# A hybrid decoder block on one core: which tile a Strassen sum is written to, when a head's output is scaled and transposed, and the order of the first casts

## The chip, the cores and the metric

One core of one Trainium2 chip runs the whole kernel in one launch. The metric is the device time of that core in microseconds (us); lower is better. The core's engines are TensorE (PE, matmuls, with PEld for its weight loads), VectorE (DVE), ScalarE (ACT), GpSimd (POOL) and SyncE (SP), which issues most DMAs.

## The reference, cut to what matters

For one layer, x of 1024 tokens by 1024, all float32:

```python
proj = x @ w_in                        # [q | f | i | og | pool_v | gate_a | gate_b]
a = HGRN2(q, f, i) -> per-head RMSNorm * sigmoid(og) -> @ w_a
b = per-group linear(causal_mean_w(pool_v) - pool_v) * pool_scale
mix = (sigmoid(gate_a) * a + sigmoid(gate_b) * b) @ w_out
x = LN(alpha * x + mix)
x = LN(alpha * x + relu(x @ w_up)^2 @ w_down)
```

HGRN2 is a gated recurrence of 8 heads with a state of 128 by 128: `S_t = diag(f_t) S_{t-1} + k_t v_t^T`, `o_t = S_t^T q_t`. The change touches the product with `w_in`, the recurrence's outputs and the pairs of `w_a`.

## The kernel before

**Products.** Every float32 product is made of three matmuls: an operand is split into a high part (float32r, a cast on ScalarE, `w_part` L245 by `split` L124, L126) and a low part (source minus high, on VectorE, L127), and hi·hi, hi·lo and lo·hi are summed in PSUM (`prod` L207, matmuls L212, L214 and L215). A product over 512 rows is four times three matmuls of 128x128 by 128x512.

**Pairs.** `pair` (L267) makes two output blocks of 128 columns for both halves of the tokens by a Strassen scheme (Winograd's form): 7 products in place of 8. The tokens' sums (a11, a12, a22, s1 to s4) lie split in SBUF all the time. The weights come as four raw blocks b11, b21, b12, b22 (128x4x128, 256 KB each, `loaded_blocks` L231, loads L223) and a fifth tile t from the same ring of six buffers (`block_tile` L217). On VectorE: T3 = b22 − b12 in t (L284), T2 = t + b11 (L301), T1 = b22 − T2 (L316), T4 = b21 − T2 (L309). Each is split and used by one product, in the order b11, b21, T2, T3, T1, T4, b22 (with `twin`, for the pairs of `w_a`: T3, T4, T2, T1 in the middle). What a tile holds decides when its buffer comes free for the next pair's load. Evictions of the products go over ScalarE (`copied`, L275) and VectorE (`added`, L279).

**Start.** Twelve idle products (L433), then the transposes of the first tokens (`transposed` L166, matmul L170; `first_tokens` L183), their splits (`in_parts` L173, cast L131, low part L132), and the first block of weights in four rows (`parts` L495 by `split`), which come by three DMAs: row 1, row 2, rows 3 and 4. `onto_chain` (L507) runs the first product row by row (L501 to L503). Ahead of them stands a small block on the lower bounds `lb` and the gains `g_neg` (L440 to L449), with one exponential (L443).

**Recurrence beside the products.** TensorE's order is written out by hand (`manual_schedule`): after every product `run` (L379) takes one turn of the generator `recurrence` (L1037). The other engines' orders come from a scheduler, which takes the order of emission, the dependences and its own times. Per head there are two halves of 512 tokens, 8.5 turns for each half. In turn 0 of a half stand `outputs` of the half before (L1010: the load of og L618, the products, squares L1022, root L1023 with its table load, reciprocal L1024, scaling by four ScalarE instructions L1026) and the keys and scores of this half. In turn `TURN_BACK` = 4 stand `turn_outputs` of the half before (L1028: four transposes L1032, the gate L1034 into og's tile, then `put_output` L632), the `states` of this half (L993) and the load of the next half's values. The other turns each take a piece of `prepare` (L881). `put_output` stores og's tile with SyncE (L636, L638) and, for the heads whose sums need it, with accumulating DMAs of GpSimd (L640, `s<-og`). The tag og has one buffer, so the next half's load of og (L618, on SyncE) waits for all of these. At the end of the recurrence, turns also take products of the pool's weights (`pool_products` L737, by `beside` L788), whose weight parts are split into tiles of the recurrence's tags (tD, tE, tF, og).

Of the kernel before, what the change touches and what calls it, by code (L numbers as in the profile page):

```python
# [12 lines left out]
AF = mybir.ActivationFunctionType  # L13
ALU = mybir.AluOpType
# [9 lines left out]
CH = HALF // P  # L24
# [3 lines left out]
LINE = 16  # L28
NW = 10
PER_HALF = 8.5  # L30
TURN_BACK = 4
TURNS_AHEAD = 3
ORDER = (
    ("inputs", 1), ("pooled", 0), ("inputs", 2), ("gates", 0), ("output_gates", 2), ("inputs", 3), ("pooled", 1),
# [17 lines left out]
def tile_hybrid_block(  # L52
# [52 lines left out]
    def f(t):  # L105
        return t.bitcast(F32)
# [17 lines left out]
    def split(src, tile_of):  # L124
        hi, lo = tile_of(), tile_of()
        A.copy(hi, src)  # L126
        V.tensor_sub(lo, src, f(hi))  # L127
        return hi, lo

    def split_into(t, src):  # L130
        hi = A.copy(t[:, 0], src)  # L131
        return V.tensor_sub(t[:, 1], src, f(t[:, 0])), hi  # L132
# [22 lines left out]
    r = [None] * 8  # L155
    xp = {name: [None] * CH for name in ("a11", "a12", "a22", "s1", "s2", "s3", "s4")}

    made_last, made_hi = {}, {}

    @contextmanager  # L160
    def behind_parts(name):
# [10 lines left out]

    def in_parts(name, kp, src):  # L173
        xp[name][kp] = act_tile()
        made_last[name], made_hi[name] = (i.ins for i in split_into(xp[name][kp], src))


    xt = [[None] * CH for _ in range(3)]
# [1 line left out]
    def minus_sum(out, a, b):  # L180
        V.scalar_tensor_tensor(out, a, -1.0, b, ALU.mult, ALU.subtract)
# [60 lines left out]
    def w_tile():  # L242
        return wq.tile([P, CH, P], F32R, tag="w", name=nm("w"), bufs=NW)

    def w_part(src):  # L245
        return split(src, w_tile)

    n_c = [0]

# [17 lines left out]
    def pair(raw, rooms, takes, pz_tag="pj", twin=False, pc_tag="pj", turned=False):  # L267


        b11, b12, b21, b22, t = raw if len(raw) == 5 else (*raw, None)  # L270
        c, ps = {}, {}

        def copied(room, ps):
            t = room()
            A.copy(t, ps)  # L275
            return t

        def added(t, ps):
            V.tensor_add(t, t, ps)  # L279
            return t  # L280

        def make_t3():
            c["t"] = block_tile() if t is None else t
            V.tensor_sub(c["t"], b22, b12)  # L284

        def t3():
            if twin:
                make_t3()
            return w_part(c["t"])

        def t2():
            if not twin:
                make_t3()
                make_t2()
            return w_part(b11)

        def make_t2():
            if turned:
                minus_sum(b11, c["t"], b11)
            else:  # L300
                V.tensor_add(b11, c["t"], b11)  # L301

        def t4():
            if twin:
                make_t2()
            if turned:
                minus_sum(b21, b11, b21)
            else:
                V.tensor_sub(b21, b21, b11)  # L309
            return w_part(b21)  # L310

        def t1():
            if turned:
                minus_sum(b12, b22, b11)
            else:
                V.tensor_sub(b12, b22, b11)  # L316
            return w_part(b12)

        def p1(w):
            ps["a"] = ps_tile()  # L320
            prod(ps["a"], w, "a11", True)
            c[11] = copied(rooms[0], ps["a"])

        def p2(w):
            if pz_tag == "pj":
                ps["z"] = ps_tile()
            ps["c"] = ps_tile(pc_tag, 4 if pc_tag == "pj" else 2)
            prod(ps["c"], w, "a12", True)

        def p7(w):  # L330
            if pz_tag != "pj":
                ps["z"] = ps_tile(pz_tag, 2)
            prod(ps["z"], w, "s3", True)
            with tc.high_priority(PRIO):
                takes[0](added(c[11], ps["c"]))
                c[22] = copied(rooms[2], ps["z"])

        def p6(w):
            prod(ps["a"], w, "s2", False)
            with tc.high_priority(PRIO):  # L340
                c[21] = copied(rooms[1], ps["a"])
                if twin:
                    takes[2](added(c[21], ps["z"]))

        def p4(w):
            prod(ps["z"], w, "a22", False)
            if not twin:
                with tc.high_priority(PRIO):
                    takes[2](added(c[21], ps["z"]))

        def p5(w):
            prod(ps["a"], w, "s1", False)
            with tc.high_priority(PRIO):
                takes[3](added(c[22], ps["a"]))

        def p3(w):
            prod(ps["a"], w, "s4", False)
            with tc.high_priority(PRIO):
                takes[1](ps["a"])

        def t0():
            return w_part(b11)

        def b_21():
            return w_part(b21)

        def b_22():
            return w_part(b22)

        middle = (  # L370
            ((t3, p7), (t4, p4), (t2, p6), (t1, p5)) if twin else ((t2, p6), (t3, p7), (t1, p5), (t4, p4))
        )
        return tuple(
            ((operand,), ((operand, product),)) for operand, product in ((t0, p1), (b_21, p2), *middle, (b_22, p3))
        )
# [48 lines left out]
    with tc.tile_pool(name="xr", bufs=8, side="right", reuse_waits="tile") as xr:  # L424
# [12 lines left out]
        lb = const.tile([P, 8], F32, name="lb")  # L437
        one_lb = const.tile([P, 8], F32, name="one_lb")
        e01 = const.tile([P, 16], F32, name="e01")
        V.tensor_max(lb, prm[:, 0:8], prm[:, 8:16])  # L440
        V.tensor_sub(e01[:, 0:8], prm[:, 0:8], lb)
        V.tensor_sub(e01[:, 8:16], prm[:, 8:16], lb)
        A.activation(e01, e01, AF.Exp)  # L443
        V.tensor_add(lb, e01[:, 0:8], e01[:, 8:16])
        V.reciprocal(lb, lb)
        V.tensor_mul(lb, lb, e01[:, 0:8])
        V.tensor_scalar(one_lb, lb, -1.0, 1.0, ALU.mult, ALU.add)
        g_neg = e01[:, 0:8]
        V.tensor_scalar_mul(g_neg, g_col, -1.0)  # L449
        x_rows = [xr.tile([P, CH, D], F32, name=f"x{u}", bufs=1) for u in range(2)]  # L450
        for t in range(8):
            r[t] = x_rows[t // CH][:, t % CH]
# [42 lines left out]
        def parts(rows):  # L495
            return [split(row, row_tile) for row in rows]
# [59 lines left out]
            put(0, 1, c, t)  # L556

        first_tokens("a11", "tr", "tr", "hg", "hg")
        w = parts(b11)
        first_tokens("a12", "tr")  # L560
        onto_chain(w, "a11", True, copied(c11, c_late))
        with behind_parts("a11"):
            w = parts(b21)
# [81 lines left out]
    with tc.tile_pool(name="tmp", bufs=1, side="right", reuse_waits="tile") as tmp:  # L645
# [224 lines left out]
        def chunk(c):  # L870
            return slice(c * P, (c + 1) * P)
# [4 lines left out]
        class Half:  # L876
# [133 lines left out]
            def outputs(self):  # L1010

                self.og = loaded(ogd[self.h][self.u], lambda: tt("og"))
                o = ps_tile("hg", 2)
                for c in range(CH):
                    w, prev = chunk(c), self.prev(c)
                    PE.matmul(o[:, w], att[:, c], self.v[:, c], start=True, stop=prev is None)
                    if prev is not None:
                        PE.matmul(o[:, w], self.qi[:, w], prev, start=False, stop=True)
                ss = small("ss", [P, CH])
                self.on = on = tt("tH")  # L1020
                for c in range(CH):
                    A.activation(on[:, chunk(c)], o[:, chunk(c)], AF.Square, accum_out=ss[:, c : c + 1])  # L1022
                A.activation(ss, ss, AF.Sqrt, bias=eps_rms, scale=1.0 / P)  # L1023
                V.reciprocal(ss, ss)  # L1024
                for c in range(CH):
                    A.activation(on[:, chunk(c)], o[:, chunk(c)], AF.Copy, scale=ss[:, c : c + 1])  # L1026

            def turn_outputs(self):  # L1028

# [7 lines left out]
        def recurrence():  # L1037

            def half(n, before):
                return Half(*divmod(n, 2), before) if n < 2 * HEADS else None  # L1040

            now, old, at = half(0, None), None, 0.0
            now.load()
            for _ in now.prepare():
                yield
            for _ in range(TURNS_AHEAD):
                yield
            for n in range(2 * HEADS + 1):
                if old:
                    old.outputs()  # L1050
                if now:
                    now.turn_keys()
                    now.scores()
                yield
                if now:
                    now.far_queries()
                nxt = half(n + 1, now) if now else None
                pieces = nxt.prepare() if nxt else iter(())
                at += PER_HALF
                for turn in range(1, round(at) - round(at - PER_HALF)):  # L1060
                    if turn == TURN_BACK:
                        if old:
                            old.turn_outputs()
                        if now:
                            now.states()
                        if nxt:
                            nxt.load()
                    else:
                        next(pieces, None)
                    yield  # L1070
                for _ in pieces:
                    pass
                now, old = nxt, now
# [456 lines left out]
```

## Time and profile before

| what | us |
| --- | --- |
| three runs | 1464.39, 1465.24, 1468.95 (median 1465.24) |
| profiled execution | 1466.59 |
| its span, first to last instruction | 1464.9 |
| TensorE busy / weight loads | 1435.5 / 1188.4 |
| VectorE / ScalarE / GpSimd busy | 1100.1 / 759.0 / 107.6 |
| mean granted TensorE clock | 0.996 |

How to read the rows: in a timeline, start, duration, engine, line, operation, tiles as out<-in; in brackets the idle time of the engine ahead of the instruction and what ended it. In the list of waits: engine and line, what they waited for, total us, times, longest. An engine with q (SPq) is its queue of instructions. Tiles go without their numbers. In the row of a DMA the last number is the median us from issue to landing. TensorE's matmuls overlap in the rows, so their pace is read from start to start.

### The profile page before, as it was taken

The numbers are of one execution on the slowest core, as the hardware profiler recorded it, in microseconds if no ns is written. First come the engines' busy times: TensorE is split into PE (matmuls) and PEld (weight loads), VectorE is DVE, ScalarE is ACT, GpSimd is POOL, SyncE is SP. The second block draws the span as 40 slices with busy tenths as digits, with TensorE's granted clock in tenths as the row PEclk, the third lists the DMA queues.
The fourth block names the chain that finished last, engine by engine and source line by source line (L and its number), as shares of the span: only waits on it lengthen the run. The fifth ranks groups of instructions, "written<-read, shape, count | busy, mean of one in ns | idle before, by whom it ended". The sixth has DMA issues, their size and how long they took to land.

```text
span 1464.9 us, 20840 instructions
## 1 busy us (share of the span) xinstructions
PE 1435.5 (98%) x7377; PEld 1188.4 (81%) x7377; DVE 1100.1 (75%) x1807; ACT 759.0 (52%) x1383; POOL 107.6 (7%) x288
## 2 busy tenths in 40 slices
PE   8999999999999999999999999999999999999997
PEld 7788888788878888877788878888888888888886
DVE  4967886796797796477985598666666787777977
ACT  5545566655755655555542366555556443333435
POOL 0002011211211210000002100000000100000000
PEclk9999999999999999999999999999999999999999
DMA  7142245345435546788673135444447774445422
GB/s 259 58 137 87 73 126 169 80 134 155 109 87 146 142 116 184 211 300 286 204 232 113 61 99 180 144 154 148 157 148 261 280 262 142 166 132 170 129 72 115
DMA packets 187161, 228.15 MB, mean 156 GB/s; under 512 B 12176, under 2 KB 110512, under 8 KB 187056
## 3 DMA queue, kind: packets, MB, share of 16 engines
q1 hardware_dynamic: 181088, 212.91, 43.9%
q0 software_dynamic: 5184, 11.54, 4.0%
q10 hardware_dynamic: 784, 2.38, 0.5%
q8 instruction: 58, 0.95, 0.3%
q14 instruction: 47, 0.39, 0.1%
HBM read 149.70 MB, written 77.07 MB: 155 GB/s over the span
## 4 chain that ended last, share of the span: by engine, by line
PE 87%; DVE 6%; DMA 4%; issue 1%; ACT 1%; SPq 0%; DVEq 0%; POOL 0%; ACTq 0%
PE ps_pj L212 15%; PE ps_pj L215 14%; PE ps_pj L214 14%; PE ps_pj L1412 4%; PE ps_pj L1413 4%; PE ps_pj L1411 4%; PE ps_pj L114 2%; PE ps_pj L113 2%; PE ps_pj L115 2%; PE ps_tr L1412 1%; PE ps_tr L1413 1%; PE ps_tr L1411 1%; PE ps_sc L215 1%; DVE w L127 1%; PE ps_hg L215 1%
## 5 line engine op out<-in xcount | busy, mean ns | idle before, releaser
L212 PE MATMUL ps_pj<-act,w 128*128 128x512 f32 x1068 | 420.2, 395 | 10.8 <-ACT c L275 3.3
L215 PE MATMUL ps_pj<-act,w 128*128 128x512 f32 x1068 | 415.7, 391 | 1.3 <-DVE w L127 1.3
L214 PE MATMUL ps_pj<-act,w 128*128 128x512 f32 x1068 | 415.0, 390 | 0.0
L126 ACT CAST w<-raw 128x512 fp32r<-128x512 f32 x310 | 192.5, 622 | 278.1 <-PE ps_pj L214 201.7
L127 DVE TENSOR_TENSOR w<-raw,w 128x512 fp32r<-128x512 f32 x310 | 212.1, 686 | 92.8 <-ACT w L126 87.6
L212 PEld LDWEIGHTS ps_pj<-act,w 128*128 128x128 f32 x1068 | 200.7, 188 | 56.9 <-ACT c L275 4.6
L215 PEld LDWEIGHTS ps_pj<-act,w 128*128 128x128 f32 x1068 | 200.8, 188 | 45.2 <-DVE w L127 2.6
L214 PEld LDWEIGHTS ps_pj<-act,w 128*128 128x128 f32 x1068 | 200.8, 188 | 40.8 <-DVE act L132 0.2
L1373 ACT CAST act<-act 128x1024 fp32r<-128x1024 f32 x66 | 66.9, 1050 | 109.0 <-issue 35.0
L279 DVE TENSOR_TENSOR c<-c,ps_pj 128x512 f32<-128x512 f32 x95 | 64.8, 682 | 39.1 <-PE ps_pj L215 35.6
L1374 DVE TENSOR_TENSOR act<-act,act 128x1024 fp32r<-128x1024 f32 x66 | 79.5, 1220 | 18.5 <-ACT act L1373 17.4
L1413 PE MATMUL ps_pj<-act,act 128*128 128x512 f32 x240 | 93.0, 389 | 0.0
L1412 PE MATMUL ps_pj<-act,act 128*128 128x512 f32 x240 | 93.0, 389 | 0.0
L1411 PE MATMUL ps_pj<-act,act 128*128 128x512 f32 x240 | 92.5, 389 | 0.0
L275 ACT COPY c<-ps_pj 128x512 f32<-128x512 f32 x96 | 55.8, 581 | 3.1 <-issue 1.8
L284 DVE TENSOR_TENSOR raw<-raw,raw 128x512 f32<-128x512 f32 x43 | 29.6, 690 | 33.2 <-DMA raw<-in_w_in_dram 28.8
L1411 PEld LDWEIGHTS ps_pj<-act,act 128*128 128x128 f32 x240 | 45.0, 188 | 9.4
L1412 PEld LDWEIGHTS ps_pj<-act,act 128*128 128x128 f32 x240 | 45.0, 188 | 9.4
L1413 PEld LDWEIGHTS ps_pj<-act,act 128*128 128x128 f32 x240 | 45.0, 188 | 9.3
L1282 ACT ACTIVATE c<-c 128x512 f32<-128x512 f32 x61 | 38.5, 632 | 1.7
L1281 ACT ACTIVATE c<-c 128x512 f32<-128x512 f32 x46 | 29.1, 632 | 15.0 <-DVE c L279 15.0
L1367 DVE TENSOR_TENSOR act<-act,ps_pj 128x512 f32<-128x512 f32 x45 | 30.1, 682 | 6.0 <-PE ps_pj L1413 5.7
(416 smaller groups left out, 2680.5 us busy)
## 6 DMA issues: line engine op xcount, KB each, us to landing
h<-c SPq DMA_DIRECT2D x106, 256.0 KB, 2.7
raw<-in_w_in_dram SPq DMA_DIRECT2D x100, 256.0 KB, 3.3
act<-h SPq DMA_DIRECT2D x78, 256.0 KB, 3.0
draw<-in_w_down_dram SPq DMA_DIRECT2D x16, 1024.0 KB, 7.6
raw<-in_w_up_dram SPq DMA_DIRECT2D x56, 256.0 KB, 2.8
hf<-h SPq DMA_DIRECT2D x34, 256.0 KB, 3.0
s<-og POOLq DMA_DIRECT2D x28, 256.0 KB, 6.1
v<-v SPq DMA_DIRECT2D x16, 256.0 KB, 3.3
```

The costliest lines, as they stand in the source:

```text
L126: A.copy(hi, src)
L127: V.tensor_sub(lo, src, f(hi))
L212: PE.matmul(ps, wh[:, k], th, start=first and k == 0, stop=False, skip_group_check=True)
L214: PE.matmul(ps, wh[:, k], tl, start=False, stop=False, skip_group_check=True)
L215: PE.matmul(ps, wl[:, k], th, start=False, stop=k == CH - 1, skip_group_check=True)
L275: A.copy(t, ps)
L279: V.tensor_add(t, t, ps)
L1373: A.copy(hi, src)
L1374: V.tensor_sub(lo, src, f(hi))
L1411: PE.matmul(ps, hh[:, w], wh, start=fresh and n == 0, stop=False, skip_group_check=True)
L1412: PE.matmul(ps, hh[:, w], wl, start=False, stop=False, skip_group_check=True)
L1413: PE.matmul(ps, hl[:, w], wh, start=False, stop=n == M - 1, skip_group_check=True)
```

## The change

Three edits.

1. In `pair`, T2 is written over b12 (its last reader until then was T3) and no longer over b11, and T1 into t's tile and no longer over b12; T4 and T1 read T2 from b12's tile. The number of instructions is the same.
2. The scaling of a half's outputs (four times L1026) is emitted in turn 2 (`TURN_SCALE`), behind the last cast of weights that was emitted, in place of turn 0; the transposes, the states and the load of values come in turn 5 in place of 4.
3. At the start only two rows of the first block are split before the first tokens; rows 3 and 4 are split behind the parts of the second and the fourth of the tokens' tiles, and the block on `lb` and `g_neg` stands behind the tokens' parts.

```diff
-TURN_BACK = 4
+TURN_BACK = 5
+TURN_SCALE = 2
...
+    last_hi = [None]
+
     def w_part(src):
-        return split(src, w_tile)
+        hi, lo = w_tile(), w_tile()
+        last_hi[0] = A.copy(hi, src).ins
+        V.tensor_sub(lo, src, f(hi))
+        return hi, lo
...
-            return w_part(b11)
+            return w_part(b12)
 
         def make_t2():
             if turned:
-                minus_sum(b11, c["t"], b11)
+                minus_sum(b12, c["t"], b11)
             else:
-                V.tensor_add(b11, c["t"], b11)
+                V.tensor_add(b12, c["t"], b11)
 
         def t4():
             if twin:
                 make_t2()
             if turned:
-                minus_sum(b21, b11, b21)
+                minus_sum(b21, b12, b21)
             else:
-                V.tensor_sub(b21, b21, b11)
+                V.tensor_sub(b21, b21, b12)
             return w_part(b21)
 
         def t1():
             if turned:
-                minus_sum(b12, b22, b11)
+                minus_sum(c["t"], b22, b12)
             else:
-                V.tensor_sub(b12, b22, b11)
-            return w_part(b12)
+                V.tensor_sub(c["t"], b22, b12)
+            return w_part(c["t"])
...
         first_tokens("a11", "tr", "tr", "hg", "hg")
-        w = parts(b11)
+        w = parts(b11[:2])
+        for row, kp in zip(b11[2:], (1, 3)):
+            lo_done, hi_done = made_kp["a11", kp]
+            with tc.issue_after(lo_done), tc.issue_after(hi_done):
+                w += parts([row])
+        with behind_parts("a11"):
+            V.tensor_max(lb, prm[:, 0:8], prm[:, 8:16])
...
+            A.activation(e01, e01, AF.Exp)
...
         first_tokens("a12", "tr")
...
-                for c in range(CH):
-                    A.activation(on[:, chunk(c)], o[:, chunk(c)], AF.Copy, scale=ss[:, c : c + 1])
+                self.o, self.root = o, ss
+
+            def scale_outputs(self):
+
+                with tc.issue_after(last_hi[0]):
+                    for c in range(CH):
+                        w = chunk(c)
+                        A.activation(self.on[:, w], self.o[:, w], AF.Copy, scale=self.root[:, c : c + 1])
...
                 for turn in range(1, round(at) - round(at - PER_HALF)):
+                    if turn == TURN_SCALE and old:
+                        old.scale_outputs()
                     if turn == TURN_BACK:
```

In the changed kernel the lines of the recurrence stand 11 further down up to the scaling and 17 from the transposes on: T3 is L290, the cast and the low part of weights L250 and L251 (others L127 and L128), the reciprocal L1035, the scaling L1043, the gate L1051.

More of the change, by code (lines that the diff above doesn't have):

```diff
@@ L156, in tile_hybrid_block @@
     xp = {name: [None] * CH for name in ("a11", "a12", "a22", "s1", "s2", "s3", "s4")}
-    made_last, made_hi = {}, {}
+    made_last, made_hi, made_kp = {}, {}, {}
     @contextmanager
@@ L174, in in_parts @@
         xp[name][kp] = act_tile()
-        made_last[name], made_hi[name] = (i.ins for i in split_into(xp[name][kp], src))
+        made_last[name], made_hi[name] = made_kp[name, kp] = [i.ins for i in split_into(xp[name][kp], src)]
     xt = [[None] * CH for _ in range(3)]
@@ L439, in tile_hybrid_block @@
         e01 = const.tile([P, 16], F32, name="e01")
[L440 to L449, printed above, removed]
         x_rows = [xr.tile([P, CH, D], F32, name=f"x{u}", bufs=1) for u in range(2)]
@@ L558, in tile_hybrid_block @@
         first_tokens("a11", "tr", "tr", "hg", "hg")
-        w = parts(b11)
+        w = parts(b11[:2])
[5 more added lines that the diff above has]
+            V.tensor_max(lb, prm[:, 0:8], prm[:, 8:16])
+            V.tensor_sub(e01[:, 0:8], prm[:, 0:8], lb)
+            V.tensor_sub(e01[:, 8:16], prm[:, 8:16], lb)
+            A.activation(e01, e01, AF.Exp)
+            V.tensor_add(lb, e01[:, 0:8], e01[:, 8:16])
+            V.reciprocal(lb, lb)
+            V.tensor_mul(lb, lb, e01[:, 0:8])
+            V.tensor_scalar(one_lb, lb, -1.0, 1.0, ALU.mult, ALU.add)
+            g_neg = e01[:, 0:8]
+            V.tensor_scalar_mul(g_neg, g_col, -1.0)
         first_tokens("a12", "tr")
```

## The prediction

> **What bounds the kernel now.** I read the page's busy shares and chain first, then what TensorE (PE) waited for, then the timeline around each of those waits.
>
> ```profile
> PE 1435.5 (98%) x7377; PEld 1188.4 (81%) x7377; DVE 1100.1 (75%) x1807; ACT 759.0 (52%) x1383; POOL 107.6 (7%) x288
> PE 87%; DVE 6%; DMA 4%; issue 1%; ACT 1%; SPq 0%; DVEq 0%; POOL 0%; ACTq 0%
> ```
>
> TensorE is the bound: busy 98% of the span and 87% of the chain that ended last. The change moves no matmul out of the program: in both instruction orders TensorE has the same 6149 rows. So it can only gain or lose where TensorE stands still or runs at a slower clock. Those places, with the engine that released them:
>
> ```profile
> PE ps_pj L212 <- ACT c L275: 3.3, 3, 1.6
> PE ps_pj L212 <- ACT w L126: 2.7, 2, 2.2
> PE ps_pj L212 <- DVE f L279: 2.0, 2, 1.3
> PE ps_pj L501 <- ACT act L131: 2.0, 1, 2.0
> PE ps_pj L212 <- ACT f L275: 1.5, 1, 1.5
> ```
>
> Columns: total us, times, longest. These are single events of 1 to 2 us. L501 is the first product of the kernel, the L275 and L279 rows are in the recurrence, and L126 (2.2) is its end. The steady pace, and three of the events:
>
> ```profile
> 431.24 0.39 PE L214 MATMUL ps_pj<-act,w 128*128 128x512 f32 x1
> 431.46 0.39 PE L215 MATMUL ps_pj<-act,w 128*128 128x512 f32 x1
> 433.32 0.50 PE L212 MATMUL ps_pj<-act,w 128*128 128x512 f32 x1 [1.47 <-ACT f L275]
> 437.62 0.50 PE L212 MATMUL ps_pj<-act,w 128*128 128x512 f32 x1 [1.29 <-DVE f L279]
> 319.77 0.50 PE L212 MATMUL ps_pj<-act,w 128*128 128x512 f32 x1 [0.74 <-DVE f L279]
> ```
>
> Start to start is about 0.227 us (431.24 to 431.46), so a product of 12 matmuls takes 2.72 us. The step 431.46 to 433.32 is 1.86 us, a loss of 1.63. In the same way each event is read as its step less 0.227.
>
> **The change part by part.**
>
> *First rows of weights behind first tokens.*
>
> ```profile
> 7.87 0.62 ACT L126 CAST w<-b 128x512 fp32r<-128x512 f32 x1 [1.82 <-DMA b<-in_w_in_dram]
> 9.27 0.66 PE L170 MATMUL ps_sc<-ident,x 128*128 128x128 f32 x4 [1.28 <-DMA x<-in_x_dram]
> 9.76 0.60 PE L170 MATMUL ps_hg<-ident,x 128*128 128x128 f32 x4
> 10.60 1.14 ACT L126 CAST w<-b 128x512 fp32r<-128x512 f32 x2 [2.12 <-DMA b<-in_w_in_dram]
> 11.64 0.21 ACT L443 ACTIVATE e<-e 128x16 f32<-128x16 f32 x1
> 11.76 1.05 ACT L131 CAST act<-ps_tr 128x512 fp32r<-128x512 f32 x2
> 12.38 0.50 PE L501 MATMUL ps_pj<-w,act 128*128 128x512 f32 x1 [2.02 <-ACT act L131]
> ```
>
> The transposes of the first tokens were done by 10.36, but ScalarE (ACT) stood for 2.12 us in front of the casts of rows 3 and 4, which wait for their DMA, and had the exponential next. In the changed order the four token casts come right behind row 2's cast (7.87 to 8.49). At 0.52 each (two in 1.05) the first is done near 9.1. The first product then waits only for the transposes ahead of it on TensorE, the last four from 9.76: four at the 0.123 that their predecessors took (9.27 to 9.76, four) end at 10.25. Gain: 12.38 − 10.25 = 2.1. Rows 3 and 4 are needed by the third and fourth quarters of the chain, 24 matmuls after 10.25, that is 15.7 at the earliest; their data is there at 10.60, so they are hidden. The exponential's result is used by the gates long after. The gap also costs clock:
>
> ```profile
> 12.40:16.60 4.20, 4.20 (x12) 0.59 1.05 390
> 16.60:21.00 4.40, 4.40 (x24) 1.00 1.05 387
> 13.24 0.63 PE L502 MATMUL ps_pj<-w,act 128*128 128x512 f32 x1
> 13.67 0.63 PE L501 MATMUL ps_pj<-w,act 128*128 128x512 f32 x1
> ```
>
> The windows show PE busy, granted clock (0.59 in the first), DMA share and GB/s. From 13.24 the products follow each other at 0.43 and not 0.227 until about 16.6: eight at 0.2 more, 1.6 us. The idle stretch from 10.36 to 12.38 lies just before. After the change nothing is idle from 9.27 on, so I count these 1.6 too: together **−3.7**, bounds −3.7 and −2.1.
>
> The Trainium skill (TensorE: Matmul & The Clock Gate, "What's actually happening") says that the clock is halved after an idle window of some 3.4 us and restored after a busy one, and that these windows run free of the kernel's start. The slow stretch here, 13.24 to 16.6, is as long as one such window. By that rule the stretch should go with the gap; where a window falls otherwise it could stay, and the sum would then lack the 1.6.
>
> *T2 over b12, T1 over t's tile.* No instruction is added; the tiles alone differ. b11's buffer comes free once T2 is computed, well before T4, so the next pair's b21 load is issued sooner. But T3 of the next pair needs b12 and b22, and these now wait for T1's and T4's readers, where they did before. The wait that reaches TensorE:
>
> ```profile
> DVE raw L284 <- DMA raw<-in_w_in_dram: 28.8, 16, 4.5
> SPq L618 <- DMA s<-og: 50.1, 15, 7.6
> 280.79 0.69 DVE L284 TENSOR_TENSOR raw<-raw,raw 128x512 f32<-128x512 f32 x1 [3.46 <-DMA raw<-in_w_in_dram]
> 287.94 0.88 ACT L1026 ACTIVATE tH<-ps_hg,ss 128x128 f32<-128x128 f32 x3 [0.41 <-DVE ss L1024]
> 289.36 0.50 PE L212 MATMUL ps_pj<-act,w 128*128 128x512 f32 x1 [1.62 <-ACT c L275]
> ```
>
> SyncE's queue stands at the load of the next half's og (L618) until the accumulating DMAs of the half before have landed, 50.1 us in all, and the block loads behind it stand too. VectorE then stands at T3 (3.46) and is late with everything behind: the reciprocal, hence the scaling L1026, hence the eviction L275 that TensorE needs at 289.36 (1.62 idle, and 0.16 beside it as at 433.32: 1.8 lost). In the changed order both block loads of this pair (at 277) stand ahead of the og load: T3 loses its wait of some 3 us, and this loss goes: **−1.8** (bounds −1.8 and 0).
>
> *Scale two, transposes one product later.* The scalings move little in ScalarE's list, behind the last cast of weights. The transposes, L1034, its puts and its accumulating DMAs come one product, 2.72 us, later, and with them the release of og's only buffer and SyncE's next og load. Where a block load stands behind that load, T3 is later:
>
> ```profile
> 395.58 0.69 DVE L284 TENSOR_TENSOR raw<-raw,raw 128x512 f32<-128x512 f32 x1 [0.76 <-DMA raw<-in_w_in_dram]
> 421.53 0.69 DVE L284 TENSOR_TENSOR raw<-raw,raw 128x512 f32<-128x512 f32 x1 [2.33 <-DMA raw<-in_w_in_dram]
> L638 SPq DMA_DIRECT2D s<-og x16: 339/447/764, 181.9 to 382.7; - x16
> ```
>
> At both, the changed order has one load behind the og load where there were two. That last load goes out 2.72 less one issue on SyncE later (0.45, the median of a put of this size in the last row), 2.2 to 2.3 us. It lands beside one transfer less: 256 KB at the 387 GB/s of full queues (the windows above) are 0.7. T3 is then, by this estimate, some 1.5 later. VectorE is busy without a break from there to 437, so the two evictions at 433.32 and 437.62 share one delay: **+1.5** (bounds −2.9, both losses gone, and +4.3, that is 2.7 and a slow stretch of 1.6). At 319.77 the last load falls behind puts of og that come 2.72 later, of which the slack of the load before hides more than half: **+0.5** (−0.7 to +1.1). The first of the losses on L275 has no load behind it: 0.
>
> *The end of the recurrence.* og's last DMAs free the tile into which the pool's weights are split:
>
> ```profile
> 608.97 0.74 DVE L1034 SCALAR_TENSOR_TENSOR og<-ps_tr,e,og 128x512 f32<-128x512 f32 x1
> 610.00 2.62 POOL L640 DMA_DIRECT2D s<-og  x3 [25.82 <-DVE og L1034]
> 620.52 0.69 DVE L127 TENSOR_TENSOR og<-tC,tF 128x512 fp32r<-128x512 f32 x1 [2.31 <-DMA s<-og]
> 621.51 0.39 PE L115 MATMUL ps_tr<-w,og 128*128 128x512 f32 x1
> 627.71 0.62 ACT L126 CAST tD<-tC 128x512 fp32r<-128x512 f32 x1 [3.37 <-DMA tC<-in_w_pool_dram]
> 628.90 0.50 PE L212 MATMUL ps_pj<-act,w 128*128 128x512 f32 x1 [2.16 <-ACT w L126]
> 630.30 0.50 PE L215 MATMUL ps_pj<-act,w 128*128 128x512 f32 x1 [0.67 <-DVE w L127]
> 631.69 0.63 PE L212 MATMUL ps_pj<-act,w 128*128 128x512 f32 x1
> s<-og POOLq DMA_DIRECT2D x28, 256.0 KB, 6.1
> ```
>
> Here pool products stand among the turns, so one turn is a product and six more matmuls, 2.72 + 1.4 = 4.1 us. L1034 comes at about 613.1, and if its DMAs take as long as before (608.97 to 620.52) the tile is free at 624.6 and its split done at 625.3; TensorE wants it at 621.51. That is a new wait of up to 3.8, and queued behind the split on VectorE are the next parts of weights and the evictions. Against it, the changed order casts the weights that TensorE missed at 628.90 ahead of tD's cast, so their 3.37 of waiting leaves that path: −2.2 and −0.7 (their idle time). Together 3.8 − 2.9 = +0.9 if the DMAs take as long as before, and −2.9 if they land in time; I take **0**, with the slow stretch behind them (0.63 for a matmul at 631.69, as at the start, 1.6 us) unchanged. Bounds: +3.8, and −2.9 − 1.6 = −4.5 if each DMA takes no more than the median 6.1 from its issue: three issues end near 615, plus 6.1 is 621.
>
> The Trainium skill (DMA: Bandwidth & Descriptors, "Anatomy of one DMA") prices such a DMA at 2.0 us and its bytes at 436 GB/s, 2.6 us for 256 KB. By that the new wait would not exist. The median above, 6.1, is more than twice that, and the measurement decides.
>
> What follows (states, v's load, the puts) hides under the next half's 8.5 products. The operands loaded after 675 change their order on SyncE: 0, between −2 and +2.
>
> **Sum.** −3.7 − 1.8 + 1.5 + 0.5 + 0 = **−3.5 us**. Against the profiled execution, 1466.6 (its span of 1464.9 and 1.7 around it, which stays), that is 1463.1. This one was 1.4 above the median of 1465.24, and against the median it gives **1461.7**.
>
> **The rivals.**
>
> 1. *The accumulating DMAs land at the median.* Then TensorE waits for nothing at the end: −4.5 instead of 0, a sum of −8.0, 1457.2. With the losses near 435 gone as well it is 1455 or less. For it: the median 6.1. Against: the last three, issued in 2.62 from 610.00, landed at 620.5, so the last took 7.9 or more.
>
> 2. *The later release becomes the bound* (slower). Price: each og load holds up the block loads behind it by the full 2.72. Then the 1.8 is not won, the two evictions lose 2.7 and a slow stretch of 1.6, the place at 319.77 loses 1.1 and the end 3.8: −3.7 + 4.3 + 1.1 + 3.8 = +5.5, and +2 with a late operand behind it: 1471 to 1473. It decides from the point at which the DMAs of the last half land later than 620.8, where TensorE at 621.51 misses its tile. For it: SyncE's 50.1 us at this very wait. Against: at 277 the order puts both loads ahead.
>
> 3. *The slow stretch at the start stays*, or falls elsewhere: −1.9, 1463.3. The rule on the clock above would allow it.
>
> 4. *The change does not do what it says at the start*: the first products wait for something else near 12.3, and only the rest remains: 1465.
>
> **How the numbers follow.** Forecast 0.42, rival 1 0.20, rival 2 0.17, rival 3 0.14, rival 4 0.07. A measurement of this kernel can tell about 0.3%, 4.4 us, from no change. Rival 1 and somewhat under half of the forecast's spread (its sum lies 0.9 inside that bound) are faster: 0.39. Rival 2 is slower: 0.17. The rest is within 0.3%: 0.44. The range leaves out the far ends of rivals 1 and 2: 1455 to 1470.
>
> **What would show it.** The start: first product (L497) near 10.3, no granted clock under 0.9 behind it. The waits: DVE's total for L290 under 28.8, with the 3.46 at 280 gone; SyncE's wait for s<-og longer than 50.1. Near 435: T3 and the two evictions later. At the end: VectorE's wait for s<-og, 2.3 before, several us, and the wait on L127's cast gone. The forecast is wrong if the first product is not earlier, if the DVE wait for s<-og stays near 2.3 (rival 1), or if TensorE shows new waits of over 2 us in several halves (rival 2).

## The result and the profile after

The change made the kernel slower: 1473.57 us median of 8 runs (1470.57 to 1476.92) against 1465.1 of 8 runs before (1462.62 to 1468.95), ratio 1.0055 with a 95% interval of 1.0039 to 1.0070. I had forecast 1461.7, and the time lies 3.6 above the range. The profiled execution took 1470.65, one of the two fastest, so its rows show less than the median loss: its last matmul starts 4.1 us later than before's. Its mean granted clock was 0.995, the median of the eight runs is 0.993. TensorE has 7377 matmuls in both profiles.

The start came as forecast. From the timeline of the changed kernel (weights' row 2, token casts, last transposes, first product), and its windows (PE busy, granted clock, DMA share, GB/s):

```profile
8.04 0.62 ACT L127 CAST w<-b 128x512 fp32r<-128x512 f32 x1 [2.98 <-DMA b<-in_w_in_dram]
8.57 1.06 ACT L132 CAST act<-ps_tr 128x512 fp32r<-128x512 f32 x2
9.95 0.60 PE L171 MATMUL ps_hg<-ident,x 128*128 128x128 f32 x4
10.31 0.48 PE L497 MATMUL ps_pj<-w,act 128*128 128x512 f32 x1
```
```profile
12.40:16.60 4.20, 4.20 (x21) 1.00 1.05 389
```

The first product starts at 10.31 in place of 12.38, and the clock between 12.4 and 16.6 is 1.00 in place of 0.59, with 21 matmuls in place of 12. What TensorE waits for afterwards (total us, times, longest):

```profile
PE ps_pj L213 <- ACT w L250: 8.8, 2, 7.3
PE ps_pj L213 <- ACT c L281: 4.6, 4, 2.0
PE ps_pj L213 <- ACT f L281: 1.6, 1, 1.6
PE ps_pj L213 <- DVE c L285: 1.4, 2, 1.1
PE ps_pj L213 <- DVE f L285: 0.5, 1, 0.5
```

The waits on the evictions of tile c by ScalarE (L281) did not go: 3.3 before, 4.6 now. And a single wait of 7.3 on ScalarE's cast of weights is new. It stands at the end of the recurrence:

```profile
611.54 2.63 POOL L651 DMA_DIRECT2D s<-og  x3 [25.57 <-DVE og L1051]
613.13 0.32 SPq L629 DMA_DIRECT2D c<-o  x1
613.54 0.42 SPq L629 DMA_DIRECT2D tH<-po  x1
622.09 0.62 ACT L127 CAST w<-tH 128x512 fp32r<-128x512 f32 x1 [11.45 <-DMA tH<-po]
623.28 0.80 PE L213 MATMUL ps_pj<-act,w 128*128 128x512 f32 x1 [7.29 <-ACT w L250]
```

A pooled operand (tH<-po) is loaded while the three accumulating DMAs are under way. ScalarE stands in front of its cast for 11.45 us, and the cast of weights that TensorE needs is next in ScalarE's queue. I had priced a wait here, but on another tile (og's) and on VectorE.

### The profile page after: what moved, and what is told of

It reads as the page before. It is cut to its first block, busy times and chain, and to the rows that moved or that the text cites. A ratio compares the mean times of both kernels' runs of the same rounds, so it can differ in the third digit from the quotient of the medians.

```text
span 1468.9 us, 20879 instructions
## 1 busy us (share of the span) xinstructions
PE 1435.8 (98%) x7377; PEld 1188.3 (81%) x7377; DVE 1099.8 (75%) x1807; ACT 758.7 (52%) x1383; POOL 105.5 (7%) x288
## 4 chain that ended last, share of the span: by engine, by line
PE 78%; DMA 7%; DVE 6%; issue 5%; ACT 3%; SPq 1%; POOL 0%; DVEq 0%; ACTq 0%; POOLq 0%
PE ps_pj L213 13%; PE ps_pj L215 13%; PE ps_pj L216 13%; PE ps_pj L1432 3%; PE ps_pj L1431 3%; PE ps_pj L1430 3%; DMA draw<-in_w_down_dram 2%; PE ps_pj L115 2%; PE ps_pj L114 2%; PE ps_pj L116 2%; PE ps_hg L215 1%; PE ps_sc L213 1%; PE ps_sc L215 1%; PE ps_sc L216 1%; PE ps_hg L213 1%
## 5 line engine op out<-in xcount | busy, mean ns | idle before, releaser
L213 PE MATMUL ps_pj<-act,w 128*128 128x512 f32 x1068 | 421.3, 395 | 17.4 <-ACT w L250 8.8
L250 ACT CAST w<-raw 128x512 fp32r<-128x512 f32 x303 | 187.8, 622 | 278.2 <-PE ps_pj L215 201.8
L251 DVE TENSOR_TENSOR w<-raw,w 128x512 fp32r<-128x512 f32 x303 | 207.1, 686 | 98.9 <-ACT w L250 97.2
L213 PEld LDWEIGHTS ps_pj<-act,w 128*128 128x128 f32 x1068 | 201.4, 189 | 64.7 <-ACT w L250 9.7
L281 ACT COPY c<-ps_pj 128x512 f32<-128x512 f32 x96 | 55.9, 582 | 6.6 <-PE ps_pj L216 3.3
L290 DVE TENSOR_TENSOR raw<-raw,raw 128x512 f32<-128x512 f32 x43 | 29.6, 689 | 32.8 <-DMA raw<-in_w_in_dram 27.6
L651 POOL DMA_DIRECT2D s<-og x28 | 24.9, 1162 | 144.1 <-DVE og L1051 144.1
```

What stands on the lines that cost most here:

```text
L213: PE.matmul(ps, wh[:, k], th, start=first and k == 0, stop=False, skip_group_check=True)
L250: last_hi[0] = A.copy(hi, src).ins
```

## The experiments

Ratios are against before on the same chip, with 95% intervals; the median of before in these batches was 1467.4, 1466.2, 1467.6 and 1466.6. Unless said otherwise a kernel is the changed one with the lines shown.

| kernel | median us | ratio (interval) |
| --- | --- | --- |
| start_alone | 1463.43 | 0.9970 (0.9961 to 0.9979) |
| tiles_alone | 1466.95 | 0.9995 (0.9983 to 1.0006) |
| turns_alone | 1479.19 | 1.0076 (1.0061 to 1.0090) |
| all_but_back | 1463.38 | 0.9968 (0.9957 to 0.9979) |
| last_back_4 | 1474.09 | 1.0051 (1.0036 to 1.0066) |
| last_only_5 | 1463.80 | 0.9980 (0.9970 to 0.9990) |
| no_last_puts | 1474.16 | 1.0049 (1.0035 to 1.0063) |
| back_3 | 1465.98 | 0.9994 (0.9984 to 1.0005) |
| outputs_4 | 1465.03 | 0.9983 (0.9972 to 0.9995) |
| outputs_5 | 1478.50 | 1.0066 (1.0048 to 1.0085) |
| no_adds_5 | 1461.11 | 0.9951 (0.9933 to 0.9969) |
| no_adds_4 | 1461.03 | 0.9954 (0.9938 to 0.9971) |
| plain_5 | 1463.30 | 0.9977 (0.9967 to 0.9987) |
| og_one_5 | 1476.51 | 1.0063 (1.0049 to 1.0076) |
| og_two_5 | 1474.41 | 1.0049 (1.0033 to 1.0065) |
| og_two_4 | 1473.18 | 1.0039 (1.0027 to 1.0050) |

**Which of the edits.** My first theory: the loss is the later turn, by its collision at the end of the recurrence. Rival: the tiles move the block loads.

start_alone is before with the third edit alone, tiles_alone with the first alone, turns_alone with the second alone; all_but_back is the changed kernel with

```diff
-TURN_BACK = 5
+TURN_BACK = 4
```

> Only the edit of the start. Both theories: the gap ahead of the first product and the slow clock behind it go, as in the changed kernel (first product near 10.3, no slow stretch to 16.6), and nothing else has a reason to move: 3.7 us less than before, about 1461.4. If the scheduler moves something else, the time differs from that.

> Only the edit of the tiles (T2 over b12, T1 over t's tile). Theory (the loss of the changed kernel lies in the later transposes, which meet the loads of the pool's operands at the end of the recurrence): no loss here, within 1.5 us of before, ScalarE's wait for tH<-po at the end 4 us as before. Rival (the tiles change the times of the block loads, and with them SyncE's order and the end): 5 us or more slower, with a wait of ScalarE for tH<-po of 8 us or more.

> Only the edit of the turns (scaling in turn 2, transposes, states and load in turn 5). Theory: the whole loss is here: the time of the changed kernel plus the 3.7 that the start gains there, 8 to 12 us slower than before, with one wait of TensorE of some 7 us at the end of the recurrence. Rival: at most 3 us slower, none over 4 us.

> The changed kernel with the transposes back in turn 4; the start, the tiles and the scaling in turn 2 stay. Theory: the end is as before (ScalarE's wait for tH<-po 4 us, none of 11), the start's gain stays: 1460 to 1463. Rival: still slower than before, 1468 or more.

The start gains 4.0 (1467.4 to 1463.4), the tiles give nothing that can be told from zero, the turns cost 11.8. Turn 4 in place of 5 alone takes the changed kernel to 1463.4, so the scaling in turn 2 costs nothing that can be told from zero, and the later transposes, states and load are the whole loss. The rival of the tiles falls.

**Is it the end?**

```diff
# last_back_4: the last half alone in turn 4
-                    if turn == TURN_BACK:
+                    if turn == TURN_BACK - (n == 2 * HEADS):
# last_only_5: TURN_BACK = 4, the last half alone in turn 5
+                    if turn == TURN_BACK + (n == 2 * HEADS):
# no_last_puts
-        for name in ONTO[right, u]:
+        for name in ONTO[right, u] if (h, u) != (HEADS - 1, 1) else ():
# back_3
+TURN_BACK = 3
```

> The changed kernel, with only the last half's transposes one turn earlier (turn 4); all other halves keep turn 5. Theory (the loss is one collision at the end: the last accumulating DMAs go out ahead of the load tH<-po, which then lands 8.5 us after its issue and not 4.3, and ScalarE holds the cast that TensorE needs): the wait of TensorE of 7.3 us is gone, 8 us or more faster than the changed kernel, 1463 to 1466 where before is 1467. Rival (the later turn costs in every half, by SyncE's og loads): at most 3 us better than the changed kernel.

> The counterpart: the changed kernel with turn 4 in all halves but the last, which keeps turn 5. Theory: the end is as in the changed kernel, a wait of TensorE of 6 us or more at the end, 1470 to 1476. Rival: 1463 to 1466, as with turn 4 everywhere (1463.4).

> The changed kernel without the three accumulating DMAs of the last head's second half: three sums of the operand of w_a lack that head, the work of 768 KB is left out. Turn 5 stays everywhere. Theory, if the DMAs share is the cause: the load tH<-po lands 4 to 5 us after its issue and TensorE's wait at the end falls from 7.3 to under 4: 4 us or more faster than the changed kernel. Rival (the load is late because its buffer and SyncE's queue are late, whatever the accumulations do): the wait stays at 6 us or more.

> The changed kernel with transposes, states and load in turn 3. Theory: the last accumulations go out one more turn earlier, the end has no wait of over 4 us, 1460 to 1465; if lateness in each half also costs, it is faster than with turn 4 (1463.4). Rival (the gain of turn 4 over 5 is chance of the order): anywhere up to 1475, with a new wait of several us.

The theory fell. With the last half alone moved back the kernel is as slow as the changed one (1474.1), with the last half alone late it is as fast as turn 4 (1463.8), and without the last accumulations nothing is won (1474.2), though TensorE's longest wait at the end is 3.9 and 4.2 in these two and no longer 7.3. So the lateness of the other fifteen halves costs. last_only_5 even shows the wait that I had priced at the end, and is fast all the same:

```profile
PE ps_tr L116 <- DVE og L128: 2.7, 1, 2.7
```

back_3 gains 0.06% on before (interval −0.05% to +0.16%) where turn 4 gains 0.32%: still earlier is not better, and a new wait of 4.5 us, on another sum of weights (L307), stands at the end.

In no_last_puts the wait for the pooled operand at the end is there without the last accumulations. SyncE issues the load only at 619.97, right behind another load, and it lands five us later; TensorE's wait behind this cast is 4.2:

```profile
619.55 0.32 SPq L629 DMA_DIRECT2D c<-o  x1
619.97 0.38 SPq L629 DMA_DIRECT2D tH<-po  x1
625.07 0.62 ACT L127 CAST w<-tH 128x512 fp32r<-128x512 f32 x1 [8.40 <-DMA tH<-po]
```

**Which piece, and by what means.** I went back to the place where I had counted a gain of 1.8, the pair near 277. DMA issues of the stretch 262 to 273 (count, KB each, median us to landing) and T3 (L290), first in the changed kernel:

```profile
s<-og POOLq DMA_DIRECT2D x3, 256.0 KB, 6.0
raw<-in_w_in_dram SPq DMA_DIRECT2D x2, 256.0 KB, 6.3
```
```profile
269.46 2.21 SPq L224 DMA_DIRECT2D raw<-in_w_in_dram  x2
275.97 0.34 SPq L629 DMA_DIRECT2D og<-og  x1
277.09 0.69 DVE L290 TENSOR_TENSOR raw<-raw,raw 128x512 f32<-128x512 f32 x1 [3.10 <-DMA raw<-in_w_in_dram]
285.76 0.60 ACT L281 COPY c<-ps_pj 128x512 f32<-128x512 f32 x1
286.41 0.50 PE L213 MATMUL ps_pj<-act,w 128*128 128x512 f32 x1 [2.00 <-ACT c L281]
```

The same with turn 4 (all_but_back):

```profile
s<-og POOLq DMA_DIRECT2D x3, 256.0 KB, 5.0
raw<-in_w_in_dram SPq DMA_DIRECT2D x2, 256.0 KB, 3.3
```
```profile
268.90 0.37 SPq L224 DMA_DIRECT2D raw<-in_w_in_dram  x1
271.42 0.34 SPq L629 DMA_DIRECT2D og<-og  x1
271.86 0.39 SPq L224 DMA_DIRECT2D raw<-in_w_in_dram  x1
274.98 0.69 DVE L290 TENSOR_TENSOR raw<-raw,raw 128x512 f32<-128x512 f32 x1 [1.61 <-DMA raw<-in_w_in_dram]
284.32 0.50 PE L213 MATMUL ps_pj<-act,w 128*128 128x512 f32 x1 [0.53 <-ACT c L281]
```

In the changed kernel both loads do stand ahead of the og load, as the order said. But they go out while the accumulating DMAs run, and take 6.3 us to land. The last accumulating DMA lands at 275.85. With turn 4 it lands at 271.30, and the loads take 3.3, one of them even behind the og load. T3 waits 3.10 against 1.61, and TensorE 2.00 against 0.53. New theory: the additions in DRAM slow the block loads that are in flight beside them. Four kernels for it:

```diff
# no_adds_5 (turn 5) and no_adds_4 (turn 4)
-        for name in ONTO[right, u]:
+        for name in ():
# outputs_4: turn_outputs in turn 4, states and load in turn 5; outputs_5: the other way round
-                    if turn == TURN_BACK:
-                        if old:
-                            old.turn_outputs()
+                    if turn == 4 and old:
+                        old.turn_outputs()
+                    if turn == 5:
...
```

> The changed kernel (turn 5) without any accumulating DMA: the operands s1 to s4 of w_a lack the halves that are added, 7 MB of work is left out. With turn 5 the block loads near 277 were issued beside the accumulating DMAs and landed 6.8 and 5.7 us after their issue, with turn 4 3.6 and 3.0. Theory (these collisions are the cost of turn 5): within 3 us of the same kernel with turn 4. Rival (another piece of the move, or the order that the scheduler makes of it, is the cost): 6 us or more slower than it.

> The same with turn 4, to be compared with the one before. Both theories: at or under the 1463.4 of turn 4 with its accumulations, since work is left out.

> The changed kernel with the transposes (and so og, its puts and accumulations) in turn 4, while the states and the load of values stay in turn 5. Theory: as with all three in turn 4, 1462 to 1465. Rival (the states or the values cost): 1470 or more.

> The counterpart: the transposes in turn 5, states and values in turn 4. Theory: as the changed kernel, 1470 to 1476. Rival: 1462 to 1466.

The additions are needed for the loss: without them turn 5 and turn 4 cost the same within the intervals (1461.1 and 1461.0). By which way they act, these kernels do not tell, as SyncE's wait in front of its loads falls as well, to 11.7. With them, the later transposes alone bring the loss: 1478.5 with the transposes in turn 5 and the states in turn 4, 1465.0 the other way round. In the rows, VectorE's wait at T3 is 32.5 us in outputs_5 and 20.4 in no_adds_5, and TensorE's on evictions and casts 9.4 and 8.1 in outputs_5:

```profile
DVE raw L290 <- DMA raw<-in_w_in_dram: 32.5, 17, 4.4
PE ps_pj L213 <- ACT c L281: 9.4, 5, 3.3
PE ps_pj L213 <- ACT w L250: 8.1, 3, 3.9
```
```profile
DVE raw L290 <- DMA raw<-in_w_in_dram: 20.4, 15, 2.6
276.54 0.69 DVE L290 TENSOR_TENSOR raw<-raw,raw 128x512 f32<-128x512 f32 x1 [0.50 <-DMA raw<-in_w_in_dram]
```

(The second fence is no_adds_5, with T3 near 277; its profiled execution was its slowest, 1465.64.) The total at T3 alone does not follow the loss, though: it is 27.6 in the changed kernel, 26.2 in all_but_back and 32.3 in start_alone, which is fast. Which late load reaches TensorE does not show in this total.

**Sharing, or the queue.**

```diff
# og_two_5, og_two_4 (turn 4); og_one_5 has NW = 9 alone
-NW = 10
+NW = 9
-RINGS = dict(q=3, f=4, og=1, ...)
+RINGS = dict(q=3, f=4, og=2, ...)
# plain_5
-            nc.gpsimd.dma_start(out=osd[name][kp], in_=t, accum_op=ALU.add)
+            nc.gpsimd.dma_start(out=osd[name][kp], in_=t)
```

> The changed kernel with two buffers for og and, to make room, nine buffers for split weights in place of ten. Theory by the queue (SyncE waits for og's release in front of block loads): several us faster than the same with one og buffer, within 4 us of turn 4. Theory by sharing (block loads land late beside the accumulations): as with one buffer, 8 us or more slower than turn 4.

> The control: the changed kernel with nine buffers for split weights and one for og. Both theories: as the changed kernel or a little slower, 1472 to 1480.

> Two buffers for og, nine for split weights, transposes in turn 4. By the queue: a little faster than turn 4 with one og buffer (1463.4), as there SyncE also waits 50 us for the accumulations; by sharing: the same or slower, 1463 to 1467.

> The changed kernel with plain stores in place of the accumulating DMAs, on the same queue and of the same size; the sums s1 to s4 then hold the last part alone. If the addition itself (its read and its slowness) is the cost: 1461 to 1465, as without these DMAs. If the transfers as such are: 1470 or more.

plain_5 is at 1463.3, so most of the cost is the addition. The transfers as such may cost some 4 us: the ratio is 0.9977 with them and 0.9951 in no_adds_5. From issue to landing (min, median, max) a DMA of 256 KB on this queue takes, in the changed kernel and then in plain_5:

```profile
DMA to landing us min/median/max: 3.9/6.0/9.2
```
```profile
DMA to landing us min/median/max: 2.6/4.1/7.0
SPq L629 <- DMA s<-og: 25.1, 14, 5.0
```

SyncE's wait for them falls too, from 48.0 to 25.1, so plain_5 alone does not part the two ways. The kernels with two og buffers were to do it and did not. The second buffer left SyncE's wait at 53.5 (54.1 in og_one_5), and og_two_4 is 10 us slower than turn 4 with ten weight buffers, against both expectations. Nine weight buffers are a change of their own: in all three kernels TensorE stops for 2.6 us near 63, ahead of the recurrence, as here in og_two_4, and all_but_back has no such stop. Turn 4 with nine weight buffers and one for og was not run, so og_two_4 says nothing on the queue:

```profile
SPq L629 <- DMA s<-og: 53.5, 16, 9.2
63.32 0.50 PE L498 MATMUL ps_pj<-w,act 128*128 128x512 f32 x1 [2.61 <-DVE w L128]
```

The traces do tell something. Of the block loads (raw<-in_w_in_dram) of the changed kernel, ten went out while an addition was under way, and their median from issue to landing is 5.8 us; the 40 between 180 and 640 us that met none have 3.1. In plain_5 nine went out beside a plain store, with 4.0. Among the kernels with ten weight buffers that keep the additions (no_last_puts all but three), the five slow ones (the changed kernel, turns_alone, last_back_4, no_last_puts, outputs_5) have 10 to 13 such loads, the seven others 5 to 9. SyncE's wait for the additions does not part them: 48.0 in the changed kernel, 48.3 in turns_alone and 59.0 in outputs_5, against 50.1 before and 50.6 in all_but_back. So sharing is the likelier way, but no kernel has tried it with the queue held still.

**What the slow clock adds.** The same stop of TensorE costs more where a slow clock follows it. Near 260 in last_back_4 the mean granted clock over six us around a stop of 1.99 is 0.72; near 286 in the changed kernel it is 1.00 around a stop of 2.00 (PE busy, granted clock, DMA share, GB/s):

```profile
260.24 0.50 PE L213 MATMUL ps_pj<-act,w 128*128 128x512 f32 x1 [1.99 <-ACT c L281]
258.50:264.50 6.00, 4.26 (x12) 0.72 0.30 87
```
```profile
285.50:291.50 6.00, 5.09 (x22) 1.00 0.27 87
```

What decides between the two these runs do not show. The mean granted clock of every run is on record, and one less this clock, times the span, is an estimate of the time that it costs: 10.3 us (median of the runs) in the changed kernel and 5.1 in all_but_back, 11.1 in outputs_5 and 6.6 in outputs_4, 8.9 in turns_alone and 7.3 in before. So by this estimate between about a seventh and a half of the loss is slow clock, and not the waits themselves.

## Why the prediction was wrong

**Right:** the start. I gave −3.7 with the slow clock counted; start_alone gains 4.0 (0.3% of 1467, interval 0.21% to 0.39%). The rule of the Trainium skill (TensorE: Matmul & The Clock Gate, "What's actually happening"), by which the slow stretch goes with the idle window, agrees with the 1.00 after 12.4, and rival 3 falls. Luck has a part in it: in tiles_alone, which keeps the stop (1.98), the granted clock is 1.00 from 12.4 to 16.6, so the 1.6 is not lost in every execution. That the tiles do nothing for T3 was right as well (0.9995), and so was the scaling at nothing (all_but_back against start_alone).

**The step that failed** is the price of the later additions, first in "T3 loses its wait of some 3 us, and this loss goes: −1.8". I read from the order that the loads stand ahead of the og load, and took them to land as if nothing ran beside them. The next step of the sum said that og's DMAs come 2.72 us later, and I let that count only through SyncE's queue; the end stood at 0. The runs showed another way: near 277 the loads beside the additions land after 6.3 us in place of 3.3, T3 still waits 3.10 (3.46 before), and T3, the reciprocal, the scaling and the eviction each come 2.1 us later than in all_but_back, to 2.00 us of TensorE (1.62 before, 0.53 in all_but_back). Nothing of the 1.8 was won. With that the sign of the move was lost: its terms were −1.8 + 1.5 + 0.5 + 0 = +0.2, and it measured +11.8 alone (turns_alone against before), and +13.5 for the transposes by themselves (outputs_5 against outputs_4). This one place is 1.5 us of it; the other stops I have not followed back to a load one by one.

**The end** I set at 0, up to +3.8. In the changed kernel's trace it holds a wait of 7.29, with a mean clock of 0.57 from 620 to 628; before, it holds waits of 2.16 and 0.67, with 0.79 from 628 to 636. The tile was not the one that I named. That the last accumulations cause the loss is refuted by no_last_puts; plain_5 and no_adds_5 still have waits of 5.6 and 2.9 there on the same cast, and are fast. How much of the loss lies there can be read from the starts of the same matmul on L212 (L213), as TensorE takes the products in the same order. Against all_but_back the changed kernel is 0.4 us behind ahead of the recurrence (93.25 and 92.88), 5.1 just before the end (611.70 and 606.62), 8.5 behind it (656.40 and 647.92) and 9.2 at the last matmul of this line. For turns_alone against before these are 0.3, 4.9, 11.7 and 11.3, for outputs_5 against outputs_4 0.5, 12.2, 15.2 and 14.4. So in single traces the end takes 3 to 7 us in place of 0, and the earlier halves the rest. How the end hangs on the earlier halves stays open.

**Near 435** I expected T3 1.5 later. In the changed kernel's trace T3 waits 1.59 there in place of 2.33, and TensorE's two waits are 1.64 and 0.55, against 1.47 and 1.29, so the loss of +1.5 did not come, and the one at 319.77 is gone.

**Rival 2** had the right sign, size (1471 to 1473) and origin, the later accumulations, with 0.17. Its path, the og load on SyncE, is at most a part: near 277 the loads were late though the og load stood behind them, and SyncE's wait for the additions, which I had expected to grow past 50.1, is 48.0. Rivals 1 and 4 are excluded by all of this.

**A faster version.** all_but_back and start_alone both stand 4 us under before, and cannot be told apart; the edit of the start alone is the simpler one.

## What to carry to other kernels

When a step that ends in DMAs is moved, ask not only who waits for them but which loads will be in flight beside them, and price these at the landing times seen under such a collision. A wait that seems settled by the order of issue can come back as a longer transfer. Of several edits in one change, the small clean one (an engine's queue at the start) could be read from rows, but for the clock behind the stop; a move by one turn in a schedule that is tuned for its collisions could not.

## What the runs showed of the hardware that I had not expected

A DMA of 256 KB from SBUF that adds to DRAM took 6.0 us (median from issue to landing) where a plain store on the same queue took 4.1, and loads of 256 KB that went out beside such additions took 5.8 (median of ten in the changed kernel) where those that met none took 3.1. In before's trace the stop of TensorE ahead of the first product cost nearly as much in clock (1.6 of 3.7 us) as in idle time: one gap of 2 us, and behind it 4.2 us at a mean of 0.59. In tiles_alone the same gap had full clock behind it:

```profile
12.16 0.50 PE L501 MATMUL ps_pj<-w,act 128*128 128x512 f32 x1 [1.98 <-ACT act L131]
12.40:16.60 4.20, 4.20 (x19) 1.00 1.05 394
```
